# Reordering the first microseconds of a one-core encoder layer: second input tile on ScalarE's queue, weights fetched behind the first tile

## The chip, the cores and the metric

One core of one Trainium2 chip runs the whole layer as one program. The metric is the device time of one execution in microseconds. The times before are three: 921.67, 923.3 and 923.6 us, median 923.3 us.

## The reference

The kernel computes one layer of a hybrid encoder on x of 512 tokens by 1024 features, all in float32:

```python
h = rms_norm(x, mix_norm_pre)
proj = h @ w_in                     # split into xa, ga, q, k, v, f, g_a, g_b
y_a = gelu(ga) * rg_lru(causal_dwconv(xa))
y_b = forgetting_attention(q, k, v, f)
merged = sigmoid(g_a) * (y_a @ w_proj_a) + sigmoid(g_b) * (y_b @ w_proj_b)
x = x + rms_norm(merged @ w_out)
h = rms_norm(x, ffn_norm_pre)
up = causal_dwconv(h @ w_up)
x = x + rms_norm((gelu(gate) * val) @ w_down)
```

The change lies wholly in the first line and in the first products of the second: `rms_norm(x)`, its transposition, and the first four 128-column blocks of `xa`.

## The kernel before

**Split products.** A float32 product is made of three products of a reduced type: each operand is split into a high part (`wh`, `hh`) and the remainder (`wl`, `hl`), and TensorE adds high by high, high by low and low by high into one accumulator. A weight block of 128 x 1024 is a `Split`: its constructor issues the fetch of the raw block on SyncE's queue (line 166), `hi()` is one cast on ScalarE (line 172), `lo()` one subtraction (line 175), in the prologue on GpSimd.

**The prologue** (lines 544 to 661) stands under a manual schedule: every engine and every queue gets its instructions in the order in which the lines stand in the program. It works on four token tiles of 128 rows (`xts[0]` to `xts[3]`) and the first four weight blocks (`us[0]` to `us[3]`). For a tile `t`:

- the fetch of x: tiles 0 and 1 in two halves of 512 columns each (line 557), tiles 2 and 3 whole (line 560), all on SyncE's queue; the gains go on ScalarE's queue (line 552);
- `sumsq(t)`: two squares with a running sum on ScalarE, their sum on VectorE, then a square root on ScalarE and a reciprocal on VectorE (lines 583 to 586, 229, 231); `sumsq_whole(t)` is the same with one square over the whole tile and no sum on VectorE (line 591);
- `scaled(t, g)`: half `g` of the tile times its scale and the gain, on VectorE (line 596). The gain lies in PSUM, broadcast to all rows by products of TensorE with a row of ones (line 575);
- `turn(t, g)`: four transpositions on TensorE (line 238), which fill the features `k` = 4g to 4g+3 of the columns of tile `t`;
- `evac_hi(t, g)`: the cast into `hh` on ScalarE (line 242); `evac_lo(t, g)`: the remainder into `hl` on VectorE (line 246).

`spin(n)` issues n products of the identity with itself into an accumulator that isn't in use yet (line 570). Nobody reads them.

`half(i, lo, hi)` makes the products of weight block `i` with the token columns `lo` to `hi`: for each `k` high by high (line 612) and high by low (line 613), then for each `k` low by high (line 615). `half(0, 0, 256)` is the first real work of TensorE: it needs tiles 0 and 1 in all features, and weight block 0. `half(1, 0, 256)`, the transpositions of tiles 2 and 3, and the other halves follow.

Behind the prologue (from line 664) the order is made by the framework's planner, which lists instructions by priority as their inputs come ready. There the gate blocks, the convolution and the scan follow, then gates, attention, output projection and the feed-forward part.

Of the kernel before, what the change touches and what calls it, by code (L numbers as in the profile page):

```python
# [8 lines left out]
F32 = mybir.dt.float32  # L9
# [7 lines left out]
P = 128  # L17
S = 512
D = 1024
KD = D // P  # L20
NT = S // P
# [42 lines left out]
def kernel(  # L64
# [15 lines left out]
    nc = tc.nc  # L80
    act, dve, pool, pe = nc.scalar, nc.vector, nc.gpsimd, nc.tensor
# [17 lines left out]
    def bank(name):  # L99
        return pspools[-1].tile([P, 512], F32, tag="ps", name=name)  # L100

    xv = x.rearrange("(t p) d -> p t d", p=P)
    ov = out.rearrange("(t p) d -> p t d", p=P)

    HALVES = (slice(0, 512), slice(512, 1024))
# [48 lines left out]
    class Split:  # L154


        def __init__(self, src, shape, name, pl=None):
            n = 1
            for d in shape:
                n *= d  # L160
            self.shape = shape
            pl = pl or wpool
            self.raw = wpool.tile([P, n], F32, tag="raw", name=f"raw_{name}", padded_shape=[P, 1024])
            self.wh = pl.tile([P, n], F32R, tag="wh", name=f"wh_{name}", padded_shape=[P, 1024])
            self.wl = pl.tile([P, n], F32R, tag="wl", name=f"wl_{name}", padded_shape=[P, 1024])
            nc.sync.dma_start(self.raw, src)

        def shaped(self, a):
# [8 lines left out]
        def parts(self):  # L177
            return self.shaped(self.wh), self.shaped(self.wl)

    def cols(w, i):  # L180
        return w[i], (KD, P)
# [4 lines left out]
    order = [(f"xa{t}", *cols(w_in, B_XA + t)) for t in range(TR)]  # L186
# [24 lines left out]
    def unit(name, ahead=2):  # L211

        i = where[name]
        fetch(i + ahead)
        return ready.pop(name)
# [11 lines left out]
    def rstd_of(ss, name):  # L227
        sd = small.tile([P, 1], F32, tag="sd", name=f"sd_{name}")
        act.activation(out=sd, in_=ss, func=AF.Sqrt, bias=epst, scale=1.0 / D)
        rs = small.tile([P, 1], F32, tag="rs", name=f"rs_{name}")  # L230
        dve.reciprocal(rs, sd)
        return rs

    def turn_block(xn, t, g, name):
        pt = bank(f"tr_{name}_{t}_{g}")
        for i in range(4):
            k = 4 * g + i
            pe.transpose(pt[:, i * P : (i + 1) * P], xn[:, k * P : (k + 1) * P], ident)
        return pt.rearrange("p (a b) -> p a b", a=4)

    def turned_hi(pv, t, g, ah):
        return act.copy(ah[:, 4 * g : 4 * g + 4, t * P : (t + 1) * P], pv)

    def turned_lo(pv, t, g, ah, al):
        dst = (slice(None), slice(4 * g, 4 * g + 4), slice(t * P, (t + 1) * P))
        return dve.tensor_tensor(out=al[dst], in0=pv, in1=ah[dst].bitcast(F32), op=ALU.subtract)
# [35 lines left out]
    hh = hpool.tile([P, KD, S], F32R, name="hh")  # L282
    hl = hpool.tile([P, KD, S], F32R, name="hl")
# [189 lines left out]
    with ExitStack() as rg:  # L473
        rt, ixt, tt = {}, {}, {}
        last_act = [None]
        with ExitStack() as r0:
# [68 lines left out]
            with tc.tile_pool(name="pre", bufs=2, side="right", reuse_waits="tile") as pre:  # L545
                after = ExitStack()
# [3 lines left out]
                gone = pre.tile([1, D + P], F32, name="gone", bufs=1)  # L550
                pool.memset(gone[:, D:], 1.0)
                act.dma_start(gone[:, :D], gains[0:1, :])
                act.activation(out=warm, in_=epst, func=AF.Sqrt)
                xts = [pre.tile([P, D], F32, tag="xt", name=f"xt{t}", bufs=NT) for t in range(NT)]
                for t in range(2):
                    for c in HALVES:
                        nc.sync.dma_start(xts[t][:, c], xv[:, t, c])
                us = [Split(*order[t][1:], order[t][0]) for t in range(2)]
                for t in range(2, NT):
                    nc.sync.dma_start(xts[t], xv[:, t])  # L560
                us += [Split(*order[t][1:], order[t][0]) for t in range(2, NF)]
# [2 lines left out]
                pss = [bank(f"xa{t}") for t in range(NF)]  # L564
# [3 lines left out]
                def spin(n):  # L568
                    for i in range(n):
                        pe.matmul(pw[:, P * (i % 4) : P * (i % 4) + P], ident, ident, start=True, stop=True)  # L570

                spin(4)
                pgain = [bank(f"gain{i}") for i in range(2)]
                for i in range(2):
                    pe.matmul(pgain[i], gone[:, D:], gone[:, 512 * i : 512 * i + 512], start=True, stop=True)
# [3 lines left out]
                def sumsq(t):  # L579
                    xns[t] = pre.tile([P, D], F32, tag="xn", name=f"xn{t}")  # L580
                    s2 = small.tile([P, 2], F32, tag="s2", name=f"s2_p{t}")
                    for i, c in enumerate(HALVES):
                        act.activation(out=xns[t][:, c], in_=xts[t][:, c], func=AF.Square, accum_out=s2[:, i : i + 1])
                    ss = small.tile([P, 1], F32, tag="ss", name=f"ss_p{t}")
                    dve.tensor_tensor(out=ss, in0=s2[:, 0:1], in1=s2[:, 1:2], op=ALU.add)
                    rss[t] = rstd_of(ss, f"p{t}")

                def sumsq_whole(t):
                    xns[t] = pre.tile([P, D], F32, tag="xn", name=f"xn{t}")
                    ss = small.tile([P, 1], F32, tag="ss", name=f"ss_p{t}")  # L590
                    act.activation(out=xns[t], in_=xts[t], func=AF.Square, accum_out=ss)
                    rss[t] = rstd_of(ss, f"p{t}")

                def scaled(t, g):
                    c = HALVES[g]
                    dve.scalar_tensor_tensor(out=xns[t][:, c], in0=xts[t][:, c], scalar=rss[t], in1=pgain[g],
                                             op0=ALU.mult, op1=ALU.mult)

                def turn(t, g):
                    ptr[t, g] = turn_block(xns[t], t, g, "p")  # L600

                def evac_hi(t, g):
                    lasts[0] = turned_hi(ptr[t, g], t, g, hh)

                def evac_lo(t, g):
                    lasts[1] = turned_lo(ptr[t, g], t, g, hh, hl)

                def half(i, lo, hi):
                    wh, wl = us[i].parts()
                    ps = pss[i][:, lo:hi]  # L610
                    for k in range(KD):
                        pe.matmul(ps, wh[:, k], hh[:, k, lo:hi], start=k == 0, stop=False)
                        pe.matmul(ps, wh[:, k], hl[:, k, lo:hi], start=False, stop=False)
                    for k in range(KD):
                        pe.matmul(ps, wl[:, k], hh[:, k, lo:hi], start=False, stop=k == KD - 1)

                sumsq(0)
                scaled(0, 0)
                sumsq(1)
                us[0].hi()  # L620
                us[0].lo(pool)
                scaled(1, 0)
                turn(0, 0)
                spin(3)
                turn(1, 0)
                scaled(0, 1)
                turn(0, 1)
                evac_hi(0, 0)
                evac_lo(0, 0)
                scaled(1, 1)  # L630
                turn(1, 1)
                evac_hi(1, 0)
                evac_lo(1, 0)
                evac_hi(0, 1)
                evac_lo(0, 1)
                evac_hi(1, 1)
                evac_lo(1, 1)
                half(0, 0, 256)
                us[1].hi()
                us[1].lo(pool)  # L640
                sumsq_whole(2)
# [6 lines left out]
                us[2].lo(pool)  # L648
                us[3].hi()
                us[3].lo(pool)  # L650
                half(1, 0, 256)
                for t in (2, 3):
                    for g in range(2):
# [95 lines left out]
        for u in range(4):  # L749
            w = unit(f"v1_{u}")  # L750
# [8 lines left out]
        for t in range(TR):  # L759
            gas[t] = bank(f"ga{t}")  # L760
            w = unit(f"ga{t}")
# [83 lines left out]
        for step, (e, half) in enumerate(PA_ORDER):  # L845
            if half == 0:
                pps[e] = bank(f"pa{e}")
            wh, wl = unit(f"pa{e}_{half}", min(2, len(PA_ORDER) - step))
            for i in range(5):
                k = 5 * half + i  # L850
# [110 lines left out]
    with ExitStack() as at:  # L961
# [3 lines left out]
        def halves(ps, name):  # L965
            hi = apool.tile([P, S], F32R, tag=f"{name[0]}h", name=f"h_{name}", bufs=1)
            lo = apool.tile([P, S], F32R, tag=f"{name[0]}l", name=f"l_{name}", bufs=1)
            rounded.append(act.copy(hi, ps))
            dve.tensor_tensor(out=lo, in0=ps, in1=hi.bitcast(F32), op=ALU.subtract)
            return hi, lo  # L970
# [97 lines left out]
        q, k = halves(pq, "q0"), halves(pk, "k0")  # L1068
        fetch(where["k1"])
        prev = None  # L1070
        for p in range(KD):
# [9 lines left out]
            if p < KD - 1:  # L1081
                pk = bank(f"k{p + 1}")
                project(pk, behind(f"k{p + 1}"), hh, hl)
                q, k = halves(pq, f"q{p + 1}"), halves(pk, f"k{p + 1}")
# [325 lines left out]
    with man2:  # L1410
# [145 lines left out]
        for t in range(2):  # L1556
            a = at_[2] + 2 + t
# [116 lines left out]
```

## Time and profile before

| | before |
|---|---|
| median of three runs | 923.3 us (921.67 to 923.6) |
| the profiled execution | 923.54 us |
| its span, first to last instruction | 921.8 us |
| TensorE busy | 908.2 us, 5834 matmuls |
| VectorE, ScalarE, GpSimd busy | 723.0, 598.4, 218.5 us |

The 1.7 us between the profiled execution's time and its span lie before the first and after the last instruction. All starts below are microseconds from the start of the span. A row of the timeline gives start, busy time, engine, line, operation, output and inputs, shape and count; in brackets stands the idle time of that engine before it and who ended it. A row of the chain of waits gives start, length and what the time went into.

### The profile page before, as it was taken

What the parts mean: (1) busy time and instruction counts of PE and PEld (TensorE: products, weight loads), DVE (VectorE), ACT (ScalarE), POOL (GpSimd) and SP (SyncE); (2) the same over time, 40 slices, a digit from 0 to 9 for tenths busy, and PEclk for the clock granted to TensorE, in tenths of its full rate; (3) what the DMA queues carried; (4) which work ended last, traced back from release to release, by engine and by line L of the source; (5) the groups of instructions that cost most, each with busy time, mean ns of one, the idle gap of its engine ahead of it and who ended that gap; (6) DMA issues with size and microseconds to landing.
All of it is one profiled execution on the core that took longest, in us unless ns stands there. A gap on an engine that the chain in (4) does not pass through costs nothing.

```text
span 921.8 us, 15768 instructions
## 1 busy us (share of the span) xinstructions
PE 908.2 (99%) x5834; PEld 803.9 (87%) x5834; DVE 723.0 (78%) x1185; ACT 598.4 (65%) x1033; POOL 218.5 (24%) x281
## 2 busy tenths in 40 slices
PE   9999999999999999999999999999999999999996
PEld 7988888878899987888888889999999999978885
DVE  5866369638767657889868588999999999889897
ACT  7555495433467656676654386688888888677664
POOL 4134345434111112112104100042323323100001
PEclk9999999999999999999999999999999999999999
DMA  7677679989977776335415554288898988799764
GB/s 274 217 233 203 171 181 271 249 235 192 202 183 183 186 261 239 111 136 167 157 62 168 203 186 140 51 209 225 221 234 206 239 206 210 226 372 324 239 203 140
DMA packets 71615, 187.07 MB, mean 203 GB/s; under 512 B 7217, under 2 KB 27489, under 8 KB 71154
## 3 DMA queue, kind: packets, MB, share of 16 engines
q1 hardware_dynamic: 47360, 127.33, 40.8%
q0 software_dynamic: 23888, 58.20, 29.3%
q8 instruction: 46, 0.75, 0.3%
q10 hardware_dynamic: 290, 0.53, 0.1%
q14 instruction: 31, 0.25, 0.1%
HBM read 150.69 MB, written 35.73 MB: 202 GB/s over the span
## 4 chain that ended last, share of the span: by engine, by line
PE 93%; DMA 2%; DVE 2%; issue 1%; ACT 1%; POOL 0%; SPq 0%; DVEq 0%; ACTq 0%; POOLq 0%
PE up L408 7%; PE up L406 7%; PE up L405 7%; PE dn L1398 4%; PE dn L1396 4%; PE dn L1397 4%; PE pa L218 2%; PE ga L219 2%; PE ga L218 2%; PE pa L220 2%; PE pa L219 2%; PE ga L220 2%; PE q L218 2%; PE k L218 2%; PE wo L1137 2%; PE pb L219 2%
## 5 line engine op out<-in xcount | busy, mean ns | idle before, releaser
L1282 DVE SCALAR_TENSOR_TENSOR u<-up,cpt,u 128x511 f32<-128x511 f32 x96 | 71.2, 744 | 2.6 <-ACT u L1276 0.9
L353 POOL DMA_DIRECT2D ml<-raw_up x41 | 35.3, 861 | 154.8 <-ACT ml L352 78.7
L1396 PE MATMUL dn<-wh_dn,ah 128*128 128x512 f32 x168 | 65.5, 390 | 0.5 <-ACT ah L1370 0.5
L1398 PE MATMUL dn<-wh_dn,al 128*128 128x512 f32 x168 | 65.6, 390 | 0.0
L1397 PE MATMUL dn<-wl_dn,ah 128*128 128x512 f32 x168 | 65.4, 389 | 0.0
L405 PE MATMUL up<-sh,th 128*128 128x256 f32 x252 | 60.5, 277 | 0.4 <-DVE up L424 0.4
L406 PE MATMUL up<-sl,th 128*128 128x256 f32 x252 | 60.4, 276 | 0.0
L175 DVE TENSOR_TENSOR wl_dn<-raw_dn,wh_dn 128x1024 fp32r<-128x1024 f32 x42 | 51.6, 1228 | 8.7 <-ACT wh_dn L172 8.7
L172 ACT CAST wh_dn<-raw_dn 128x1024 fp32r<-128x1024 f32 x42 | 44.1, 1050 | 17.9 <-issue 11.6
L317 DVE TENSOR_TENSOR tl<-t,th 128x1024 fp32r<-128x1024 f32 x42 | 51.1, 1217 | 1.8 <-ACT th L387 1.8
L1276 ACT ACTIVATE u<-up,cpt 128x512 f32<-128x512 f32 x48 | 36.9, 778 | 19.6 <-PE up L408 10.8
L405 PEld LDWEIGHTS up<-sh,th 128*128 128x128 f32 x252 | 47.3, 188 | 0.5 <-DVE up L424 0.5
L387 ACT CAST th<-t 128x1024 fp32r<-128x1024 f32 x42 | 43.9, 1044 | 5.7 <-DVE t L317 2.5
L406 PEld LDWEIGHTS up<-sl,th 128*128 128x128 f32 x252 | 47.3, 188 | 0.0
L1290 POOL TENSOR_TENSOR yf<-u,u 128x512 f32<-128x512 f32 x23 | 30.5, 1329 | 63.9 <-issue 45.9
L405 PE MATMUL up<-h2h,mh 128*128 128x256 f32 x168 | 40.3, 276 | 0.0
L406 PE MATMUL up<-h2l,mh 128*128 128x256 f32 x168 | 40.3, 276 | 0.0
L408 PE MATMUL up<-sh,tl 128*128 128x256 f32 x252 | 38.9, 276 | 0.0
L1398 PEld LDWEIGHTS dn<-wh_dn,al 128*128 128x128 f32 x168 | 31.5, 188 | 7.5 <-DVE al L317 0.8
L1396 PEld LDWEIGHTS dn<-wh_dn,ah 128*128 128x128 f32 x168 | 31.5, 188 | 7.2 <-ACT ah L1370 0.9
L996 ACT ACTIVATE P<-P,mx 128x384 f32<-128x384 f32 (+2 forms) x64 | 35.2, 552 | 3.7 <-DVE mx L991 2.8
L1397 PEld LDWEIGHTS dn<-wl_dn,ah 128*128 128x128 f32 x168 | 31.5, 188 | 6.5
(717 smaller groups left out, 3255.3 us busy)
## 6 DMA issues: line engine op xcount, KB each, us to landing
raw_up<-in_w_up_dram SPq DMA_DIRECT2D x48, 512.0 KB, 5.5
td<-in_w_down_dram POOLq DMA_DIRECT2D x36, 512.0 KB, 6.0
raw_dn<-td SPq DMA_DIRECT2D x24, 512.0 KB, 4.8
B<-cnd POOLq DMA_DIRECT2D x16, 640.0 KB, 5.6
ml<-raw_up POOLq DMA_DIRECT2D x20, 512.0 KB, 5.3
raw_dn<-in_w_down_dram SPq DMA_DIRECT2D x18, 512.0 KB, 4.3
raw_wo<-in_w_out_dram SPq DMA_DIRECT2D x16, 512.0 KB, 4.2
td<-td POOLq DMA_DIRECT2D x12, 512.0 KB, 12.2
```

The source lines that it names most:

```text
L172: act.copy(self.wh, self.raw)
L175: engine.tensor_tensor(out=self.wl, in0=self.raw, in1=self.wh.bitcast(F32), op=ALU.subtract)
L218: pe.matmul(dst, ah, bh, start=first, stop=False)
L219: pe.matmul(dst, ah, bl, start=False, stop=False)
L317: dve.tensor_tensor(out=out, in0=a, in1=b, op=ALU.subtract)
L405: pe.matmul(dst, wh[:, k], ah[:, k], start=first and k == 0, stop=False, skip_group_check=True)
L406: pe.matmul(dst, wh[:, k], al[:, k], start=False, stop=False, skip_group_check=True)
L408: pe.matmul(dst, wl[:, k], ah[:, k], start=False, stop=k == KH - 1, skip_group_check=True)
L1282: dve.scalar_tensor_tensor(out=c[:, s:], in0=ps[:, : S - s], scalar=col(C_CFW + 3 * e + j), in1=c[:, s:], op0=ALU.mult, op1=ALU.add)
L1396: pe.matmul(dst[t], ah[:, k, tok], wh[:, k], start=first, stop=False, skip_group_check=True)
L1397: pe.matmul(dst[t], ah[:, k, tok], wl[:, k], start=False, stop=False, skip_group_check=True)
L1398: pe.matmul(dst[t], al[:, k, tok], wh[:, k], start=False, stop=last, skip_group_check=True)
```

## The change

Five things are changed, all within the prologue:

1. Tile 1 of x is fetched whole, and on ScalarE's queue, ahead of ScalarE's warming square root; tile 0 stays on SyncE's queue in two halves.
2. The fetch of weight block 0 is held back: a copy of one column of tile 0 into the raw block, on GpSimd, goes ahead of it. So the fetch waits for tile 0, and everything that stands behind it on SyncE's queue with it.
3. Tile 0 goes ahead of tile 1: both halves of tile 0 are scaled before tile 1's, tile 1 is squared whole, and the transpositions run tile 0 first, half, half, then tile 1, half, half. The low parts `evac_lo` come after the last `scaled` on VectorE.
4. The spins are 3, 2 and 2 products instead of 4 and 3.
5. The products of block 0 with the first 256 columns are ordered by kind: eight high by high, four high by low, eight low by high, and the last four high by low.

```diff
-        def __init__(self, src, shape, name, pl=None):
+        def __init__(self, src, shape, name, pl=None, after=None):
...
+            if after is not None:
+                pool.tensor_copy(out=self.raw[:, 0:1], in_=after)
             nc.sync.dma_start(self.raw, src)
...
                 act.dma_start(gone[:, :D], gains[0:1, :])
+                xts = [pre.tile([P, D], F32, tag="xt", name=f"xt{t}", bufs=NT) for t in range(NT)]
+                for c in HALVES:
+                    nc.sync.dma_start(xts[0][:, c], xv[:, 0, c])
+                act.dma_start(xts[1], xv[:, 1])
                 act.activation(out=warm, in_=epst, func=AF.Sqrt)
-                xts = [pre.tile([P, D], F32, tag="xt", name=f"xt{t}", bufs=NT) for t in range(NT)]
-                for t in range(2):
-                    for c in HALVES:
-                        nc.sync.dma_start(xts[t][:, c], xv[:, t, c])
-                us = [Split(*order[t][1:], order[t][0]) for t in range(2)]
+                us = [Split(*order[t][1:], order[t][0], after=None if t else xts[0][:, D - 1 :]) for t in range(2)]
...
-                spin(4)
+                spin(3)
...
+                def parts(i, which, ks, start=False, stop=False):
+                    wh, wl = us[i].parts()
+                    w, a = {"hh": (wh, hh), "hl": (wh, hl), "lh": (wl, hh)}[which]
+                    for k in ks:
+                        pe.matmul(pss[i][:, :256], w[:, k], a[:, k, :256], start=start and k == 0, stop=stop and k == KD - 1)
+
                 sumsq(0)
                 scaled(0, 0)
-                sumsq(1)
+                sumsq_whole(1)
+                scaled(0, 1)
+                turn(0, 0)
+                evac_hi(0, 0)
                 us[0].hi()
                 us[0].lo(pool)
+                spin(2)
+                turn(0, 1)
+                evac_hi(0, 1)
                 scaled(1, 0)
-                turn(0, 0)
-                spin(3)
+                scaled(1, 1)
+                spin(2)
                 turn(1, 0)
-                scaled(0, 1)
-                turn(0, 1)
-                evac_hi(0, 0)
+                evac_hi(1, 0)
                 evac_lo(0, 0)
-                scaled(1, 1)
+                evac_lo(0, 1)
                 turn(1, 1)
-                evac_hi(1, 0)
+                evac_hi(1, 1)
                 evac_lo(1, 0)
-                evac_hi(0, 1)
-                evac_lo(0, 1)
-                evac_hi(1, 1)
                 evac_lo(1, 1)
-                half(0, 0, 256)
                 us[1].hi()
...
                 us[3].lo(pool)
+                parts(0, "hh", range(KD), start=True)
+                parts(0, "hl", range(KD // 2))
+                parts(0, "lh", range(KD))
+                parts(0, "hl", range(KD // 2, KD), stop=True)
                 half(1, 0, 256)
```

## The prediction

> **What bounds the kernel now.** I read the page first, for the bounding engine, and its chain of waits.
>
> ```profile
> span 921.8 us, 15768 instructions
> PE 908.2 (99%) x5834; PEld 803.9 (87%) x5834; DVE 723.0 (78%) x1185; ACT 598.4 (65%) x1033; POOL 218.5 (24%) x281
> PE 93%; DMA 2%; DVE 2%; issue 1%; ACT 1%; POOL 0%; SPq 0%; DVEq 0%; ACTq 0%; POOLq 0%
> ```
>
> TensorE is the bound. A prologue edit therefore moves the end by as much as it moves the moment at which TensorE has the first block behind it, if TensorE then runs on without new waits. Next I read the chain in the first 17 us.
>
> ```profile
> 1.19 4.20 DMA xt<-in_x_dram
> ...
> 5.41 0.73 ACT xn L583 x2
> ...
> 6.96 0.76 DVE xn L596
> ...
> 7.76 1.11 PE tr_p L238 x4
> 8.87 1.28 PE xa L570 x6
> 10.15 2.75 PE tr_p L238 x12
> 12.90 0.21 PE xa L612
> ...
> 14.39 0.29 PE xa L613
> ```
>
> The chain starts with the second half of tile 0, which ScalarE sees at 5.41. Call this moment L. From L to the first transposition at 7.76 lie 2.35 us of square, root, reciprocal and scaling. From there on the chain is TensorE's alone: four transpositions, three spins (a spin is two instructions), twelve transpositions, then products. Neither tile 1 nor the weights are on it. TensorE's timeline gives its rate.
>
> ```profile
> 3.49 3.78 PE L575 MATMUL gain<-gone 1*128 1x512 f32 x4
> 7.76 1.11 PE L238 MATMUL tr_p<-ident,xn 128*128 128x128 f32 x4 [0.49 <-DVE xn L596]
> 12.55 0.56 PE L612 MATMUL xa<-hh,wh_xa 128*128 128x256 f32 x1
> 13.34 0.41 PE L613 MATMUL xa<-hl,wh_xa 128*128 128x256 f32 x1
> 13.55 0.38 PE L612 MATMUL xa<-hh,wh_xa 128*128 128x256 f32 x1
> 13.76 0.28 PE L613 MATMUL xa<-hl,wh_xa 128*128 128x256 f32 x1
> 13.88 0.28 PE L612 MATMUL xa<-hh,wh_xa 128*128 128x256 f32 x1
> 16.19 0.28 PE L612 MATMUL xa<-hh,wh_xa 128*128 128x256 f32 x1
> 10.30:13.70 3.40, 3.40 (x17) 3.08 (x16) 2.86 (x6) 1.99 (x5) 2.01 (x1) 1.00 1.02 415
> ```
>
> Starts are 0.21 us apart until 13.76 and 0.12 after: TensorE runs at about half rate until then. (The last row, of the table by stretches, gives a granted clock of 1.00 there; it shows no throttle that early, so I go by the spacing.) At half rate one of the small instructions takes 1.28/6 = 0.213 us, and the first block's 24 products run from 12.55 until the next block's first one at 16.19.
>
> **The transposition order and the spins.** Between L+2.35 and the first product TensorE now issues 4+6+12 = 22 instructions, by rate 4.69 us, and the trace shows 12.55-7.76 = 4.79. So only 0.1 us of this stretch is waiting. The new order has 16 transpositions and four spins, 24 instructions, 5.11 us. If nothing waits, the first product comes at L+7.46, which for L = 5.41 is 12.87: **0.32 us later**. The first spin is one shorter, but that lies ahead of the gain products (3.49 to 7.27) and ends in idle time before 7.76: nothing.
>
> Does something wait? VectorE and ScalarE have these rows:
>
> ```profile
> 8.81 1.04 ACT L172 CAST wh_xa<-raw_xa 128x1024 fp32r<-128x1024 f32 x1
> 11.04 0.58 ACT L242 CAST hh<-tr_p 128x512 fp32r<-128x512 f32 x1 [0.70 <-PE tr_p L238]
> 14.36 1.06 ACT L591 ACTIVATE xn<-xt 128x1024 f32<-128x1024 f32 x1
> 16.07 1.41 DVE L596 SCALAR_TENSOR_TENSOR xn<-xt,rs_p,gain 128x512 f32<-128x512 f32 x2
> 10.99 0.74 DVE L596 SCALAR_TENSOR_TENSOR xn<-xt,rs_p,gain 128x512 f32<-128x512 f32 x1
> 13.55 0.69 DVE L246 TENSOR_TENSOR hl<-tr_p,hh 128x512 fp32r<-128x512 f32 x1 [0.35 <-ACT hh L242]
> ```
>
> A whole-tile square to the first scaling takes 16.07-14.36 = 1.71 us. Tile 1's square stands on ScalarE behind tile 0's root, so it starts at L+1.15 if tile 1 has landed. Its reciprocal stands on VectorE ahead of tile 0's second scaling, which is a new wait: that scaling now starts at L+1.15+1.71 = L+2.86, and the three left end at about L+3.6, L+4.3 and L+5.0. TensorE wants them at L+4.06 (after the first four transpositions and two spins), L+5.8 and L+6.6. All are in time, by 0.4 us at the tightest. The last scaling is done at 10.4 instead of 11.73 (10.99+0.74). ScalarE's casts of 0.58 follow each group of transpositions: the one for tile 1's first half is ready at about L+7.4, the last at about L+8.3, and the products want them at L+7.46 and, after four products, L+8.3. No wait of note at half rate.
>
> **The order by kind.** In the old order the fifth high-by-low product waited for the last `hl` (13.55+0.69 = 14.24): the chain's 0.29 at 14.39 against 0.12 beside it, 0.17 us. In the new order these four stand last and that wait is gone. From 12.87, four products at 0.213 reach 13.75, and 20 at 0.12 end at 16.15, against 16.19 now. So with L where it is, the reordering is worth **0.0, ±0.1 us**. The later start costs little, because the half-rate stretch ends at its own time.
>
> If the full rate came at 11.2, one whole stretch after 7.76, the old order would still be held to 16.1 by that last `hl`, while the new one would go through its transpositions by 12.05 and its products by 15.4: a gain of 0.65. If it came at 14.6, the new one would lose 0.2.
>
> The Trainium skill (TensorE: Matmul & The Clock Gate, Part 1) says that TensorE's clock is halved until one free-running window of about 3.4 us has been busy, with a phase that differs from run to run. The trace agrees with a step at 13.76; that the phase varies no run here shows yet.
>
> **The transfers.** SyncE and ScalarE issue, and the transfers land, so:
>
> ```profile
> 0.74 1.81 SPq L557 DMA_DIRECT2D xt<-in_x_dram  x4
> 2.60 0.91 SPq L166 DMA_DIRECT2D raw_xa<-in_w_in_dram  x2
> 3.55 1.40 SPq L560 DMA_DIRECT2D xt<-in_x_dram  x2
> 0.74 0.52 ACTq L552 DMA_DIRECT2D gone<-in_gains_dram  x1
> 1.30 1.28 ACT L553 ACT_TABLE_LOAD   x1 [1.30 <-PEq L1661]
> 3.30 0.63 ACT L583 ACTIVATE xn<-xt 128x512 f32<-128x512 f32 x1 [0.50 <-DMA xt<-in_x_dram]
> 5.41 0.63 ACT L583 ACTIVATE xn<-xt 128x512 f32<-128x512 f32 x1 [1.39 <-DMA xt<-in_x_dram]
> 7.48 0.63 ACT L583 ACTIVATE xn<-xt 128x512 f32<-128x512 f32 x1 [0.21 <-DMA xt<-in_x_dram]
> DMA to landing us min/median/max: 3.4/6.2/9.4
> ```
>
> Tile 1 is issued on ScalarE from 1.26 for about 0.7 us (SyncE's whole tiles took 1.40/2). The table load and the first square move back by that, to about 3.6; ScalarE then still waits for L, so this is free. But tile 1's 512 KB now start next to tile 0's second half (issued at 1.2), where before they stood behind it on one queue. The trace doesn't show two queues in this stretch. Bounds for L: the second half alone, right behind the first square, 4.3; all of both tiles, as today's last quarter shows, 7.48. I take a third of the way to the late end from 5.41, **L = 6.1**, since tile 0 has its first half in flight before. That is 0.7 us later; with the half-rate stretch ending where it does, the new sum loses half to two thirds of it, **+0.4 us**.
>
> The Trainium skill (DMA: Bandwidth & Descriptors, Queues, rings and completion order) has each of the 16 DMA engines go round-robin between the queues that have work. By that rule the two tiles would finish together, L near 7.4; it speaks against the change, and is the first rival.
>
> Weight block 0 is issued after L, one copy on GpSimd and SyncE's start, at about L+0.5. The last row above is for the blocks of `xa`: 3.4 us at the least. So it lands at L+3.9, and ScalarE wants it at L+4.0; a later landing has 1.1 us of cover before the cast of 1.04 holds up tile 1's casts. The old one hid entirely. Behind it on SyncE's queue block 1, tiles 2 and 3, blocks 2 and 3 and the constants are issued 3 to 4 us later too (L+0.5 against 2.60). At the 415 GB/s of the row of 10.30:13.70 each 512 KB takes 1.26 us, so with block 0 at 10.0 block 1 lands at about 11.3 and tile 2 at 12.5. Tile 2's square stands at 14.36 in the old trace, with block 1's cast of 1.04 just ahead of it, at 13.3, and move no earlier. Cover of some 2 us: nothing. If it went, block 1's cast would hold up the second block and each microsecond past it would count in full.
>
> **The sum** against the profiled 923.54: order and kinds 0.0, later tile +0.4, weights 0: 923.9. The median of the runs is 0.24 lower, so I forecast **923.7 us**. Runs before span 1.9 us, 0.2%, about what a measurement of this kernel can tell from no change; the bounds are 921.45 and 925.15.
>
> **Rivals.** *Slower: the two queues share the engines.* Place: ScalarE's second square of tile 0. Tile 0 would wait for nearly all of both tiles, L = 7.4, which is 2.0 us later; tile 1's reciprocal then holds VectorE further. It decides once L passes 6.6, where the start of steady work has moved by over a third of a 3.4 us stretch and the step to full rate can fall one stretch later, worth another 1.7. Price: 1.2 to 3 us, 924.5 to 926.3. For it: four transfers of 256 KB took until 7.48 to land. Against it: tile 0's first half has nearly landed when tile 1 starts.
>
> *Faster: tile 0 lands sooner because no weights compete.* L could fall to 4.3, 1.1 us, and the transpositions could meet the full rate, 0.65 more; if the step also comes a stretch earlier, 1.7 more. 921.9 down to 920.5. For it: 1.39 us of waiting at 5.41. Against: the weights were issued at 2.60, behind all of x on the same queue.
>
> *The planner's order behind the prologue shifts.* It works on modelled times, and these change. TensorE's waits behind the prologue:
>
> ```profile
> PE up L408 <- DMA ml<-raw_up: 0.8, 1, 0.8
> ...
> PE gate L531 <- DMA halo_h<-xl: 0.3, 1, 0.3
> ```
>
> These are the longest and the shortest of seven (0.8, 0.7, 0.5, 0.5, 0.4, 0.4, 0.3: 3.6 us). There is little to win and more to lose: 921 to 927.
>
> **How the numbers follow.** Forecast (within 0.2%) 0.46; queues sharing with an effect beyond it 0.26; tile 0 sooner 0.16; planner 0.12, two thirds slower. Faster 0.20, same 0.46, slower 0.34. The range leaves out a tenth on each side: 921.3 to 926.3; the forecast's own is 922.6 to 925.
>
> **What would show it.** Tile 0's second square: at 6.1 as I say, 4.3 or 7.4 by the rivals. First product 7.46 us after it; no wait over 0.2 before the `hl` products; `hi` of block 0 not waiting for its fetch. I am wrong if the next block's first product moves by over 1 us, or if waits appear behind the prologue.

## The result, and the profile after

| | before | after |
|---|---|---|
| median | 923.21 us (921.67 to 924.8, 14 runs) | 925.24 us (923.35 to 927.4, 14 runs) |
| ratio, 95% interval | | 1.0021 [1.0012, 1.0029] |
| profiled execution | 923.54 us | 926.22 us |
| its span | 921.8 us | 924.1 us |

The new order is slower by 2.0 us. That lies inside the forecast's range (921.3 to 926.3), but 0.09 us beyond the bound of 925.15 up to which the forecast counted as no change, and 1.5 us above the forecast itself. The page of after, the lines that answer to those shown of before:

```profile
span 924.1 us, 15764 instructions
PE 907.7 (98%) x5834; PEld 803.0 (87%) x5834; DVE 722.0 (78%) x1184; ACT 598.3 (65%) x1031; POOL 220.8 (24%) x282
PE 88%; DVE 5%; DMA 4%; issue 2%; ACT 1%; POOL 0%; SPq 0%; DVEq 0%; ACTq 0%; POOLq 0%
```

TensorE is busy no longer than before, but its share of the chain fell from 93% to 88%, VectorE's rose from 2% to 5% and that of transfers from 2% to 4%. That suggests a wait for a transfer, but such shares can't carry the reading: in the second profiles of before, without the loss, and of after, with it (both below), they stand the other way round:

```profile
PE 88%; DVE 5%; DMA 3%; issue 2%; ACT 1%; POOL 0%; SPq 0%; DVEq 0%; POOLq 0%; ACTq 0%
```
```profile
PE 93%; DMA 2%; DVE 2%; issue 1%; ACT 1%; POOL 0%; DVEq 0%; SPq 0%; ACTq 0%; POOLq 0%
```

So the place of the loss has to be looked for row by row. The chain of the first 17 us of after:

```profile
1.19 4.27 DMA xt<-in_x_dram
...
5.48 0.73 ACT xn L585 x2
...
7.03 0.76 DVE xn L598
...
7.84 1.12 PE tr_p L240 x4
...
13.04 3.17 PE xa L623 x24
16.21 0.12 PE xa L614
```

It shows no new wait in the prologue. The chain has the same links; the first product comes at 13.04, and by the timeline of TensorE the next block's first product at 16.04 (16.19 before). The prologue of this execution ends 0.15 us *earlier*. TensorE's waits over the whole span show the place of the loss; this row stood at 0.3 before:

```profile
PE gate L533 <- DMA halo_h<-xl: 2.2, 1, 2.2
```

This is the first gate block, 27 us behind the edited products. It multiplies a tile `halo_h`, which SyncE's queue fills with rows of `xh` and `xl` of neighbouring blocks (line 522). Its place in the chain of waits, in TensorE's timeline (idle before it in brackets), and in the table of two neighbouring stretches (length, then busy time of TensorE, weight loads, VectorE, ScalarE, GpSimd, then the granted clock as a share of TensorE's full speed, DMA share and GB/s):

```profile
40.80 5.54 DMA halo_h<-xl
...
46.42 0.69 PE gate L533
```
```profile
46.42 0.69 PE L533 MATMUL gate<-halo_h,gh 96*128 96x512 f32 x1 [2.17 <-DMA halo_h<-xl]
46.91 0.63 PE L220 MATMUL gate<-xh,gh 128*128 128x512 f32 x1
47.34 0.63 PE L221 MATMUL gate<-xl,gh 128*128 128x512 f32 x1
```
```profile
43.09:46.51 3.42, 1.25 (x7) 0.74 (x6) 3.20 (x5) 3.10 (x4) 1.60 (x2) 1.00 0.56 189
46.51:49.92 3.41, 3.41 (x9) 2.65 (x10) 1.99 (x3) 2.17 (x4) 0.29 (x1) 0.50 0.92 314
```

The same fetch before:

```profile
44.73 0.47 PE L531 MATMUL gate<-halo_h,gh 96*128 96x512 f32 x1 [0.34 <-DMA halo_h<-xl]
```

There are two losses. TensorE waits 1.8 us longer for the halo's low rows. And since it had worked only 1.25 of the 3.42 us up to 46.51, the next stretch is granted half the clock: products start 0.43 us apart (46.91, 47.34) instead of 0.23, which costs half of 3.41, 1.7 us. Lined up product by product, after stands 0.13 us ahead of before at the start of the first gate block and 3.29 us behind at the second, and it still does so 200 us later. In the feed-forward part 1.3 us come back; the second profile of before (below) gains as much there on the first, so that part varies by itself.

### The profile page after: what moved, and what is told of

Same layout as the page of the kernel before. It is cut to its first block, busy times and chain, and to the rows that moved or that the text cites. A ratio compares the mean times of both kernels' runs of the same rounds, so it can differ in the third digit from the quotient of the medians.

```text
span 924.1 us, 15764 instructions
## 1 busy us (share of the span) xinstructions
PE 907.7 (98%) x5834; PEld 803.0 (87%) x5834; DVE 722.0 (78%) x1184; ACT 598.3 (65%) x1031; POOL 220.8 (24%) x282
## 4 chain that ended last, share of the span: by engine, by line
PE 88%; DVE 5%; DMA 4%; issue 2%; ACT 1%; POOL 0%; SPq 0%; DVEq 0%; ACTq 0%; POOLq 0%
PE up L410 7%; PE up L408 7%; PE up L407 7%; PE dn L1410 4%; PE dn L1408 4%; PE dn L1409 4%; PE ga L222 2%; PE ga L220 2%; PE ga L221 2%; PE q L220 2%; PE k L220 2%; PE wo L1149 2%; PE pb L221 2%; PE k L222 2%; PE pb L222 2%
```

## The experiments

The instructions behind the prologue stand in the same order on every engine in both kernels, with one exception: the planner put the two fetches of gate weights on SyncE's queue (line 505) from 7.47 us forward to 1.66. So the question was what makes a transfer at 40 us land 2 us later. Suspects at that place are the *background puts*: from about 33 us on, GpSimd issues one 512 KB copy inside DRAM per unit (`background(1, u)`), each behind a one-column copy (`tick`, line 149) out of a converted weight block, which sets its time.

**The two parts of the change alone, and both kernels with the puts moved.** One kernel is the old prologue with edits 1 and 2 (the fetches), one the new prologue with the old fetches. The other two are before and after with no put in the first four units, so that the first goes out at 53 or 54 us, and two in each unit of the values' second part:

```diff
-                if t > NF:
+                if t > NF + 4:
                     background(1, u)
...
             v_mm(u, pv, w)
-            background(1, w)
+            background(2, w)
```

> The kernel before with the new fetches alone (tile 1 on ScalarE's queue, weight block 0 held back behind tile 0; the first gate weights move ahead of it on SyncE's queue as in the changed kernel), order, spins and products as before. Theory 'prologue fetch': tile 0's second square comes later than 5.4 us in most runs, and this part carries the loss: 1.5 to 2 us slower than before, about 925. Theory 'gate': the loss is at the first gate block (PE waiting at 44 to 46.5 us for the halo rows, then a stretch of half rate), set by where the halo transfer falls among the background sums; then this kernel has 0 to 2 us of it by its own luck, and tile 0's second square stays at 5.3 to 5.6. Theory 'order': this part is free, within 0.5 us of before.

> The changed kernel with the fetches of before: only order, spins and products by kind are new. Theory 'prologue fetch': within 0.5 us of before, about 923.2. Theory 'order': two more instructions at half rate and another rhythm for the clock carry the loss, 1.5 to 2 us slower. Theory 'gate': the first block ends 0.1 to 0.2 us earlier than before and the first gate block waits 0 to 2.5 us.

> The kernel before with the first four background transfers (32 to 46 us, GpSimd's queue) moved behind: they are made up by two a step in the second V part. Theory 'gate': the halo rows of the first gate block land in under 3 us, the wait of 0.3 us there goes, and the time falls by 0.3 to 1.5 us, as runs of before that had a longer wait lose it. Theories 'prologue fetch' and 'order': within 0.3 us of before.

> The changed kernel with the first four background transfers moved behind in the same way. Theory 'gate': the wait of 2.2 us and the half-rate stretch behind it go; it ends within 0.5 us of the kernel before with the same move, 2 to 3 us below the changed kernel. Theories 'prologue fetch' and 'order': it keeps the distance of about 2 us to the kernel before with the same move.

Measured against the same runs of before (median 922.72 us): fetches alone 926.13 us, 1.0034 [1.0021, 1.0048]; order alone 923.6, 1.0010 [0.9997, 1.0023]; before with moved puts 921.96, 0.9986 [0.9974, 0.9998]; after with moved puts 922.29, 0.9992 [0.9981, 1.0003]. In both kernels with moved puts the halo's low rows land in 1.9 us and TensorE has no wait there; the two differ by 0.33 us, less than either interval. So the loss needs the puts where they were. Each half of the change has the wait too: 0.8 us in the profile of the fetches alone, 2.0 us in that of the order alone. A profile shows one execution: that of order alone took 925.67 us, the second longest of twelve with a median of 923.6, so its wait need not be the usual one. The fetches alone lose more; a second reason is on show there, since weight block 0 came late for the old order and ScalarE waited for it:

```profile
9.82 1.05 ACT L174 CAST wh_xa<-raw_xa 128x1024 fp32r<-128x1024 f32 x1 [0.75 <-DMA raw_xa<-in_w_in_dram]
```

That is one row of one execution, in which the full rate came only at 16.93 us; how much of the 3 us it makes I can't say.

**When the puts go out.** Timelines of VectorE and GpSimd of before, then of after:

```profile
35.88 1.23 DVE L175 TENSOR_TENSOR wl_xa<-raw_xa,wh_xa 128x1024 fp32r<-128x1024 f32 x1 [0.22 <-issue]
35.68 0.18 POOL L149 COPY tick<-wh_xa 128x1 f32<-128x1 f32 x1 [2.13 <-ACT wh_xa L172]
36.13 0.50 POOL L127 DMA_DIRECT2D td<-in_w_down_dram  x1 [0.27 <-issue]
38.99 0.49 POOL L127 DMA_DIRECT2D td<-in_w_down_dram  x1 [0.25 <-issue]
```
```profile
35.44 1.23 DVE L177 TENSOR_TENSOR wl_xa<-raw_xa,wh_xa 128x1024 fp32r<-128x1024 f32 x1
35.55 1.17 POOL L149 COPY tick<-wh_xa 128x1 f32<-128x1 f32 x1 [2.13 <-ACT wh_xa L174]
36.65 0.50 POOL L127 DMA_DIRECT2D td<-in_w_down_dram  x1
38.85 0.49 POOL L127 DMA_DIRECT2D td<-in_w_down_dram  x1 [0.25 <-issue]
```

Before, GpSimd's copy starts first and takes 0.18 us, and VectorE's subtraction starts as it ends. After, the subtraction starts 0.11 us ahead and the copy takes 1.17 us: it ends with the subtraction (36.72 and 36.67). The second put goes out 0.5 us later, and the third then flies longer. The issues of the third put and of the halo's low rows (KB each, us to landing), before and after:

```profile
td<-in_w_down_dram POOLq DMA_DIRECT2D x1, 512.0 KB, 5.0
halo_h<-xl SPq DMA_DIRECT2D x1, 64.0 KB, 3.5
```
```profile
td<-in_w_down_dram POOLq DMA_DIRECT2D x1, 512.0 KB, 6.8
halo_h<-xl SPq DMA_DIRECT2D x1, 64.0 KB, 5.5
```

The Trainium skill (SBUF — State Buffer, Who interferes with whom) says that a VectorE instruction with two SBUF inputs contends with a GpSimd instruction that reads SBUF, that the port pair they share is an exclusive lock, and that the order of issue decides who blocks. The trace agrees, with 0.18 and 1.17 us.

The next four: before unchanged, for a second profile; before with the four ticks reading the low part; after with the four ticks reading the raw block; and after with the moved puts of above and the two gate-weight fetches held where before had them.

```diff
-        i = pool.tensor_copy(out=tick, in_=w[0].bitcast(F32)[:, 0, 0:1])
+        i = pool.tensor_copy(out=tick, in_=w[1].bitcast(F32)[:, 0, 0:1])   # xa5 to xa8: low part
...
+        i = pool.tensor_copy(out=tick, in_=w.raw[:, 0:1])                  # xa5 to xa8: raw block
```
```diff
+                with tc.issue_after(cpt_dma.ins):
                     nc.sync.dma_start(raw, rgw[:, t])
```

> The kernel before, unchanged: a second profile of its first gate block. 'Put timing' (the loss of the new order sits where the rows that the second background put moves lie beside the halo's rows, and what decides it is whether GpSimd's one-column copy ahead of that put runs before or after VectorE's subtraction): the copy for that put takes about 0.2 us again, the halo lands in about 3.5 us, TensorE waits at most 0.5 us for it, the full rate holds to the end of the kernel; ratio 1.000 within 0.001. 'Chance' (the wait at the gate comes and goes from execution to execution whatever the kernel): copy and wait may come out as in the new order, 1 us and 2 us.

> The kernel before, but GpSimd's one-column copies ahead of the four background puts of the first block's units read the low part instead of the high one, so that each put always follows VectorE's subtraction. 'Put timing': the second put is issued at 36.6 us or later (36.1 before), TensorE waits 1 to 2.5 us for the halo at the first gate block, and where that wait is over about 2 us the clock drops for one window; 924 to 926 us, ratio 1.001 to 1.003, though nothing of the prologue's new order is in it. 'Prologue' (the loss comes with the new fetches or the new order alone): as before, ratio within 0.001 of 1, wait at most 0.5 us.

> The new order, but GpSimd's one-column copies ahead of the same four puts read the block as it was fetched, so that each put goes out up to 2 us earlier and waits for neither part. 'Put timing': the put's rows have mostly passed when the halo's start at 40.8 us; wait at the first gate block 0.5 us or less, no dropped window, 922 to 923 us, ratio 0.9985 to 1.000. 'Prologue': the loss stays, about 925 us, ratio 1.002.

> The new order with the first four background puts in the second part of the values' stage, two a step, and the two fetches of the gate's weights held behind the fetch of the constants on SyncE's queue as they stood before. 'Put timing': no wait at the first gate block, as with the moved puts alone (922.3 us); the 0.5 MB less beside the first tile's rows changes the landing of tile 0 by 0.1 us at most: 921.5 to 922.5 us, ratio 0.998 to 1.000. 'Fetches share' (the gate's weights held up the first rows): tile 0's second half lands by 5.0 us and tile 1's by 6.5, and 0.5 us more is gained.

Measured, before at 922.56 us: before again 923.07, 1.0005 [0.9993, 1.0017], with tick 0.18 us and wait 0.3 as in the first profile. That speaks against 'chance'. After with raw ticks: 922.06, 0.9998 [0.9987, 1.0009], no wait; the loss is gone. The puts went out earlier than I had said, by 10 to 13 us (22.2, 23.8, 26.3, and the fourth at 34.2), so this shows that the puts' time matters, not that half a microsecond does. Held gate weights: 922.4, 0.9997 [0.9987, 1.0006], the second square of tile 0 at 5.43, as without holding them: their move does not set that square. With the puts moved too there was no loss left in this run, so it can't say whether their move causes the loss; order alone can, where they are issued at 7.28 us as before and TensorE waits 2.0 us. So their move is not needed for the wait.

Before with low ticks missed: 923.91, 1.0011 [1.0001, 1.0021], but the wait was 0.2 us, not 1 to 2.5. The edit pushed all of the puts back (35.46, 38.18, 44.51), so that the third no longer stood ahead of the halo. It was a bad test of the second put, and where its 1 us lies I did not find.

**One put at a time.** After unchanged; after with the raw tick for the second put alone; before with all four raw ticks (the first of these then also stands ahead of GpSimd's last subtraction of the prologue); before with the low tick for the second put alone (`if n == "xa6"` in place of the four names).

> The new order, unchanged: a second profile of its first gate block. 'Put timing': GpSimd's copy ahead of the second background put is held for about 1.2 us again, that put is issued 3.1 us ahead of the halo's low rows or less, TensorE waits 1.5 to 2.5 us at the first gate block; ratio 1.001 to 1.003. 'Chance': wait and copy come out as in the kernel before.

> The new order with one of GpSimd's copies changed: the one ahead of the second background put reads the block as fetched, so that this put is issued right behind the first (about 33.4 us instead of 36.65), and the other three stay. 'Put timing': the wait at the first gate block falls to 0.5 us or less and no window is dropped; 922 to 923 us, ratio 0.9985 to 1.0005. 'Third put' (the one at 38.85 us, 2 us ahead of the halo's low rows, is what holds them): the wait stays over 1.5 us.

> The kernel before with the first four background puts as early as in the new order with early puts (22 to 34 us), so that the two differ in the prologue's order alone. If the prologue gains the 0.15 us that the trace showed and nothing else of it counts: this kernel within 0.5 us of the new order with early puts (ratio 0.9998 there), no wait at the first gate block, ratio 0.9990 to 1.0005 here. If the order by itself costs time behind the prologue: this one is faster by 1 us or more.

> The kernel before with the copy ahead of the second background put reading the low part, so that it waits for VectorE's subtraction: that put is issued at 37 to 38 us (36.13 before), the first and third stay. 'Put timing': the wait at the first gate block grows from 0.3 to 1 to 4 us, ratio 1.001 to 1.004, the new order's loss without any part of the new order. 'Prologue': wait and time as before.

Measured, before at 922.09 us: after again 923.45, 1.0022 [1.0011, 1.0033]; second put early 923.55, 1.0014 [1.0005, 1.0024]; before with early puts 921.83, 1.0001 [0.9992, 1.0010]; before with the second put late 923.86, 1.0030 [1.0016, 1.0044]. TensorE's first halo product in before's second profile, in after's second, and in before with the late put:

```profile
43.55 0.47 PE L531 MATMUL gate<-halo_h,gh 96*128 96x512 f32 x1 [0.31 <-DMA halo_h<-xl]
```
```profile
45.32 0.47 PE L533 MATMUL gate<-halo_h,gh 96*128 96x512 f32 x1 [1.62 <-DMA halo_h<-xl]
```
```profile
46.20 0.77 PE L534 MATMUL gate<-halo_h,gh 96*128 96x512 f32 x1 [2.42 <-DMA halo_h<-xl]
```

The last of them is the decisive run. The old prologue, with nothing of the change in it and one put 1 us later (issued at 37.09), has the whole loss: the wait, the dropped clock, and a ratio no better than the change's. Early puts, in the same way, make the two orders equal (0.9998 and 1.0001). But moving the second put alone in the new order took the wait only to 1.2 us, between my two cases (0.5 or less, over 1.5). That put went out at 35.29 us, but took 7.2 us to land. Put beside each other, the eleven profiles with puts ahead of the halo show what goes with the wait (differences are from the unrounded times; the fourth column tells how long the put before the last one was still moving):

| kernel | last put ahead of the halo: issued, took | halo's low rows: issued, took | the put before it lands after its issue by | last put lands after the halo's issue by | TensorE's wait |
|---|---|---|---|---|---|
| before, early puts | 35.41, 5.2 | 40.83, 1.9 | -2.6 | -0.2 | 0 |
| after, early puts | 34.15, 5.7 | 39.94, 2.0 | -2.2 | -0.1 | 0 |
| before, low ticks | 38.18, 5.6 | 42.36, 2.6 | 3.0 | 1.4 | 0.2 |
| before | 38.99, 5.0 | 41.10, 3.5 | 2.4 | 2.9 | 0.3 |
| before again | 37.84, 5.0 | 39.94, 3.5 | 1.5 | 2.9 | 0.3 |
| fetches alone | 40.78, 5.2 | 42.71, 4.1 | 2.4 | 3.3 | 0.8 |
| after, second put early | 39.90, 5.9 | 41.85, 4.6 | 2.6 | 4.0 | 1.2 |
| after again | 38.30, 6.4 | 40.23, 5.0 | 3.9 | 4.5 | 1.6 |
| after | 38.85, 6.8 | 40.80, 5.5 | 4.0 | 4.9 | 2.2 |
| order alone | 39.35, 6.8 | 41.27, 5.3 | 4.0 | 4.8 | 2.0 |
| before, second put late | 38.37, 7.1 | 40.49, 5.6 | 4.2 | 5.0 | 2.4 |

From 2.9 us on, the halo's rows land 0.5 to 0.8 us after that put, whatever the prologue. The put moves in pieces of 32 KB that held an engine for 1.2 us and more each (the trace's packets), the halo in rows of 2 KB. So the wait goes with how long the last put ahead of the halo still moves. That the puts' times make or remove the wait is shown, in both orders. That this one put holds the halo's rows is argued from the table, and a rival is untested: a fetch of weights (`raw_v`, 512 KB), which stands ahead of the halo on SyncE's own queue, is late too (it lands at 42.78 us before and 44.25 after). In the same profiles the halo's rows land 1.6 to 2.5 us behind that fetch, so the put fits more closely, but no run moves the fetch alone.

What lengthens the put's flight from 5.0 to 6.8 us is shown for one lever, the second put's time in the old order. The fourth column says what goes with it in all: in the four longest flights (6.4 to 7.1 us) the put before was still moving for 3.9 to 4.2 us, in the other seven for 3.0 or less. Why it does so in the new order is open beyond the 0.5 us by which it was issued later. Open too is why VectorE starts first in the four profiles with a part of the change that keep this copy, when the order on both engines is the same.

## Why the prediction was right or wrong

**The prologue: its sum is not refuted, but its reason was partly wrong.** I started from L = 5.41, the moment at which ScalarE sees tile 0's second half, and let it go to 6.1. Six profiles of either prologue show another base (us; for each the six values, with their mean):

| | L | first product | next block's first product |
|---|---|---|---|
| old order | 5.41, 4.08, 4.23, 4.34, 4.60, 4.11: 4.46 | 12.49 | 16.19, 15.03, 17.11, 16.66, 15.92, 15.58: 16.08 |
| new order | 5.48, 5.28, 5.43, 4.84, 5.43, 5.36: 5.30 | 12.97 | 16.04, 15.50, 15.95, 15.21, 16.34, 17.11: 16.03 |

(Old: before twice, moved puts, and the three with changed ticks; new: after twice and its four variants. Of the halves, fetches alone had L at 5.50 and order alone at 5.10.) The 5.41 of the one profile that I had is the highest of the old order's six. Tile 1 beside tile 0 does cost L 0.8 us, as I said (0.7), but it ends near 5.3, not 6.1, and much of it is hidden behind something that I had not put on the chain, the gain products on TensorE. In the second profile of before they, not L, end last ahead of the first transposition:

```profile
3.50 3.78 PE L575 MATMUL gain<-gone 1*128 1x512 f32 x4
7.21 1.12 PE L238 MATMUL tr_p<-ident,xn 128*128 128x128 f32 x4
```

The first product moves by 0.48 us, and the end of the first block by -0.05 us: I had +0.4 for the transfers and 0.0 ± 0.1 for the order. Six values against six that spread over 2 us tell this end only to about ±0.9, so they don't refute the +0.4. The whole times help more: with moved puts the new order was 0.33 us slower, with early puts its ratio was no higher than the old order's. Some of the -0.05 may be luck: the full rate, whose time varies by itself, began at 12.30 us on average in these profiles of the new order, at 12.81 in those of the old. That the last `hl` no longer holds anything was right: in after no product of high by low waits.

**The steps in between: right in five profiles of six.** By the signals that I named: the first product came at L+7.56 (7.46 foretold) in after's first profile and at L+7.2 to 7.6 in four others. In the sixth (second put early) tile 1 landed only at 8.2, TensorE waited 0.89 us for tile 0's second scaling, which stands behind tile 1's reciprocal, and the first product came at L+8.7. In after's first profile the wait ahead of the first product was 0.17 us, and the cast of block 0 (9.47) did not wait for its fetch; in three others it did, by 0.6 to 1.0 us, and their first products waited 0.24 us:

```profile
5.48 0.63 ACT L585 ACTIVATE xn<-xt 128x512 f32<-128x512 f32 x1 [1.38 <-DMA xt<-in_x_dram]
7.16 1.06 ACT L593 ACTIVATE xn<-xt 128x1024 f32<-128x1024 f32 x1 [0.43 <-DMA xt<-in_x_dram]
9.47 1.05 ACT L174 CAST wh_xa<-raw_xa 128x1024 fp32r<-128x1024 f32 x1
```

**The rivals.** 'Queues share the engines' priced L at 7.4; no profile has it past 5.5. The round-robin rule beside it fared better in order than in time: in four of the six profiles of the new order tile 1, issued at 1.3, landed 4.2 to 4.7 us later, 0.4 to 0.7 us after L (in the other two after 5.8 and 6.9), so the tiles can land nearly together; but they do so at 5.5 to 6.0. Why my price of 7.4, taken from one queue with weights behind x, was too high no run shows. 'Tile 0 sooner' fails by sign: L is later. The third rival held the loss, with the right row on show (0.3 for the halo) and the wrong mechanism: the planner's order did not shift but for the two fetches named above, the time of a few transfers did. I read that row as the smallest of seven waits; it was also the one whose growth counted in full.

**The term that failed** is thus the one that is not in the sum: the condition 'if TensorE then runs on without new waits'. By my own sign ('if waits appear behind the prologue') the account of the kernel's time is wrong. That the result lies in the range all the same is luck: 925.24 lies among the prices of the slower rivals, and neither came by its mechanism. Its size, against 2.03 us measured: the wait, 2.2 and 1.6 us in two profiles against 0.3, is 1.6; a dropped stretch of 1.7 us shows in the mean granted clock (0.996 or less) of 5 of the 25 executions of the new order and of none of 104 of before run beside the experiments, 0.3; the prologue -0.05. Outside the span the new order's executions took 2.0 us and the old 1.8 (medians), 0.2, which no experiment explains. Together 2.1; with a wait read in two executions and a prologue known to ±0.9, the terms are known less well than they agree.

## What to carry to other kernels

An edit that leaves the order of all later work as it is can still shift the instant at which a background transfer starts; look for short waits on small transfers that share the engines with large ones, for they have no cover. Move the large ones away from there: with the puts elsewhere both prologues ran at 922 us, and the kernel before with moved puts (0.9986 [0.9974, 0.9998]) is the only version here whose interval lies below 1. And take the base of a sum from two executions: the first 5 us differed by 1.3 us from one to the next.

## What the runs showed of the hardware

**Half the clock after waits of about 2 us.** The granted clock changed at instants that lie whole multiples of 3.413 us apart within an execution (after: 12.38, 46.51 and 49.92), at a phase that differs from run to run: the full rate began at 13.75, 10.38, 14.89, 14.39, 11.60 and 11.85 us in six executions of the old order (that the phase varies no run had shown before). Stretches of before with the late put, of order alone and of after's second profile, columns as above:

```profile
42.57:45.98 3.41, 1.21 (x6) 0.67 (x4) 3.41 (x6) 3.05 (x4) 1.60 (x2) 1.00 0.57 185
45.98:49.40 3.42, 3.20 (x8) 2.56 (x9) 2.04 (x3) 1.84 (x4) 0.00 (x0) 0.50 0.89 311
```
```profile
43.93:47.35 3.42, 1.45 (x7) 0.92 (x6) 3.21 (x5) 3.40 (x4) 1.60 (x2) 1.00 0.53 127
47.35:50.76 3.41, 3.41 (x10) 2.67 (x9) 2.46 (x4) 2.47 (x5) 1.26 (x1) 0.50 0.86 330
```
```profile
42.10:45.51 3.41, 1.79 (x9) 1.20 (x8) 3.19 (x5) 2.66 (x4) 1.49 (x2) 1.00 0.37 116
45.51:48.92 3.41, 3.41 (x16) 2.77 (x16) 3.17 (x5) 3.20 (x5) 1.29 (x2) 1.00 0.94 320
```

A stretch with 1.21, 1.25 or 1.45 us of TensorE's work was followed by half the clock, one with 1.79 was not. The Trainium skill (TensorE: Matmul & The Clock Gate, Why this matters for your kernels) asks for gaps of no more than about 3 us; here waits of 2.0 to 2.4 us were enough, one of 1.6 was not, and the measurement decides.
